# Value products of attention given out behind the next group's transposes, the last operand's product first

## The chip, the cores and the metric

The kernel runs as one program on 1 core of one Trainium2 chip. The metric is the device time of one execution in microseconds (us); the core's five engines (TensorE for matmuls, VectorE, ScalarE, GpSimd, and SyncE, which issues DMAs) run side by side, each through its own queue of instructions in order, and wait for one another through semaphores. In the profile TensorE stands as PE (matmuls) and PEld (its weight loads), VectorE as DVE, ScalarE as ACT, GpSimd as POOL and SyncE as SP.

## The reference

One layer of a decoder with two kinds of attention side by side, 2048 tokens of width 1024, in float32. What the change touches are the two attentions, 8 heads of width 64 each:

```python
# forgetting attention (FoX), F = cumsum(log_sigmoid(forget logits))
s = einsum('bhqd,bhkd->bhqk', q_blk, k) * scale + F_blk[..., None] - F[:, :, None, :]
p = softmax(where(causal, s, -inf))
o_fox = einsum('bhqk,bhkd->bhqd', p, v)

# stick-breaking attention
z = einsum('bhqd,bhkd->bhqk', q_blk, k) * scale
log_one_minus_beta = where(strict, log_sigmoid(-z), 0.0)
rest = cumsum(log_one_minus_beta, axis=3, reverse=True) - log_one_minus_beta
a = where(strict, exp(log_sigmoid(z) + rest), 0.0)
o_sb = einsum('bhqk,bhkd->bhqd', a, v)
```

Around them: a modulated RMSNorm and one input projection that gives q, k and v of both kinds and the forget logits; after them a per-head RMSNorm, the output projection with a gated residual, a gated MLP with a causal convolution of width 3, and a last RMSNorm.

## The kernel before

**Precision.** Operands of matmuls are split into two float32r parts, a high one (a rounded copy) and a low one (what the copy left). A product is the sum of high by high, high by low and low by high, or, where a [high | low] pair is packed into the 128 rows or columns of the array, two matmuls.

**Units.** Attention works through 32 units, `units`: first the stick-breaking kind (`sb`), then the forgetting kind (`fox`); in each, 4 pairs of heads `p`; for each pair, 4 blocks `tb` of 512 queries. `attend` (from L697) runs one unit: two halves `j2` of 256 queries by two heads `hl`, so four passes of one head over 256 queries. `sb_head` (L620) takes the keys in chunks of 512 from the last to the first: per chunk and each of the two rows of 128 queries (`qi` 0 and 1) there are two matmuls for the logits (`logits`, L594, lines L596 and L597), two sigmoids on ScalarE (L630, L631) and one scan on VectorE (L636). `fox_head` (L657) first makes all logits of a row, adds the forget sums and keeps the running minimum on VectorE (L675), and takes the exponential on ScalarE (L679), for `qi` 0 and then 1.

**A group.** Both give their weights to `weighted` (L600), once per group of 256 queries by 256 keys. Its steps: four 128x128 transposes on TensorE into one PSUM bank `pt` of three (L606; three of them in a group on the diagonal); a copy on ScalarE into the high half of an operand tile `at` of three (L610); a subtraction on VectorE into its low half (L611); and four value products on TensorE (L615), for two key tiles `kk` times the high and the low half `w`. On the diagonal ScalarE also fills a quarter of `at` with zeros first (L609). The order of the transposes is `order = [(1, 0), (0, 0), (0, 1), (1, 1)]`, each pair being key tile and query row. The products of all groups of one head add up in one bank `o`: the single bank `pv`, or one of two banks `bc` in the last but one unit. There are 576 groups.

**The end of a head.** When a head's groups are through, ScalarE copies half of `o` to SBUF (L737), VectorE adds the other half to it into `oT` (L738), and after both heads `head_var` squares `oT` on GpSimd (L711) and puts off two variance matmuls (L716) by 13 steps. After both halves SyncE stores `oT` to DRAM.

**The order of work.** The program is traced by generators that yield at each group: `interleave` draws one step of attention, then as many steps of the next units' projections (`project`, lines L342 and L413) as `pace` has due, then fillers such as the modulation's remaining part (`late_mod`, L780 to L790) and, in the last two units, the first part of the output projection (`first_mix`, `first_out`, L912). From this trace a scheduler fixes the order on every engine by a simulated timeline (`schedule_with_timeline_sim=True`): of the instructions whose operands the simulation holds ready, the one traced first is issued. So a product that is traced before the next group's transposes can still stand after them. `tc.issue_after(x)` adds an order on one engine without a wait: what is traced in it stands behind `x` in that engine's queue. `sums` and `step` note the last product and the two copies of a group for such orders later (`behind`, and the first output products of the last stage).

Of the kernel before, what the change touches and what calls it, by code (L numbers as in the profile page):

```python
# [9 lines left out]
F32 = mybir.dt.float32  # L10
F32R = mybir.dt.float32r
BF16 = mybir.dt.bfloat16
AF = mybir.ActivationFunctionType
# [4 lines left out]
P = 128  # L18
# [3 lines left out]
HD = 64  # L22
# [3 lines left out]
NTB = S // TB  # L26
# [8 lines left out]
def kernel(ctx: ExitStack, tc: tile.TileContext, x, c, w_ada, b_ada, g_attn, w_in, b_fgate,  # L35
                      g_out_fox, g_out_sb, w_out, g_mlp, w_up, conv_w, conv_b, w_down, g_final, out):
    nc = tc.nc
# [3 lines left out]
    def f(t):  # L41
        return t.bitcast(F32)
# [9 lines left out]
    os_ = [[dram.tile([P, TB], F32, name=f"os{p}_{t}") for t in range(NTB)] for p in range(NPAIR)]  # L52
# [21 lines left out]
    ident = edge[:, TB - P:TB]  # L74
# [50 lines left out]
    def open_pool(name, side=None, space=None):  # L125
        st = pools[name] = ExitStack()
        kw = dict(space=space) if space is not None else {}
        return st.enter_context(tc.tile_pool(name=name, bufs=1, side=side, reuse_waits="tile", **kw))
# [8 lines left out]
    sb = open_pool("sb", side="right")  # L137
# [3 lines left out]
    def bank(pool, tag, bufs):  # L141
        return pool.tile([P, 512], F32, name=f"ps_{tag}", tag=tag, bufs=bufs)
# [4 lines left out]
    pv = lambda: bank(psb, "pv", 1)  # L147
# [55 lines left out]
    last = {}  # L203
# [13 lines left out]
    b = pv()  # L217
# [37 lines left out]
    class mod_cols:  # L255
# [6 lines left out]
        def add(self, k0, k1):  # L262
            if k0 == 0:
                self.t = px.tile([P, 2, 2 * P], F32, name="adas", tag="z", bufs=2)
                nc.vector.tensor_scalar_mul(self.t, self.w[0], cs[:, 0:1])
            for k in range(max(1, k0), k1):
                nc.vector.scalar_tensor_tensor(self.t, self.w[k], cs[:, k:k + 1], self.t, ALU.mult, ALU.add)
# [326 lines left out]
    def logits(cw, qcols, hl, Q, K):  # L594
# [2 lines left out]
        marks.append(nc.tensor.matmul(b[:, :cw], Q[:, hl, 1, qcols], K[:, hl, :cw], start=False, stop=True).ins)  # L597
        return b

    def weighted(o, kts, blk, V, hl, first, last, diag):  # L600
        b = pt()
        at = sb.tile([P, 2, 2 * 2 * P], F32R, name="at", tag="at", bufs=3)
        order = [(1, 0), (0, 0), (0, 1), (1, 1)]
        for i, (kk, qi) in enumerate(order):
            if not (diag and i == 0):
                nc.tensor.transpose(b[:, i * P:(i + 1) * P], blk(kts[kk], qi), ident)  # L606
        lo = P if diag else 0
        if diag:
            nc.scalar.activation(at[:, :, 0:P], edge[:, 0:2 * P].rearrange("p (a n) -> p a n", n=P), AF.Copy)  # L609
        copies = [nc.scalar.activation(at[:, 0, lo:], b[:, lo:], AF.Copy).ins,  # L610
                  nc.vector.tensor_sub(at[:, 1, lo:], b[:, lo:], f(at[:, 0, lo:])).ins]  # L611
        for kk, kt in enumerate(kts):
            for w in range(2):
                rhs = at[:, w].rearrange("p (s q) -> p s q", q=P)[:, 0:4:3, :] if kk else at[:, w, P:3 * P]
                m = nc.tensor.matmul(o[:, 0:2 * P], V[kt // 4][:, kt % 4, hl, :], rhs,  # L615
                                     start=first and kk == 0 and w == 0, stop=last and kk == 1 and w == 1)
        sums.append(m.ins)
        step[:] = [m.ins] + copies

    def sb_head(j, qc, hl, Q, K, V, o):  # L620
        n = (2 * j + 2 + 3) // 4
        right = [None, None]
        for ch in range(n - 1, -1, -1):
            at = []
            for qi in range(2):
                need = min(512, (2 * j + qi + 1) * P - ch * 512)
                b = logits(max(need, 2 * P), slice((qc + qi) * P, (qc + qi + 1) * P), hl, Q, K[ch])
                r = sx.tile([P, 512], F32, name="r", bufs=7)
                a = sx.tile([P, 512], F32, name="a", bufs=7)
                nc.scalar.activation(r[:, :need], b[:, :need], AF.Sigmoid)  # L630
                nc.scalar.activation(a[:, :need], b[:, :need], AF.Sigmoid, scale=-1.0)  # L631
                if right[qi] is None:
                    nc.gpsimd.affine_select(out=a[:, need - P:need], in_=a[:, need - P:need], pattern=[[-1, P]],
                                            base=-1, channel_multiplier=1, compare_op=ALU.is_ge, fill=0.0)
                rev = a[:, 0:need][:, ::-1]
                nc.vector.tensor_tensor_scan(rev, r[:, 0:need][:, ::-1], rev,  # L636
                                             0.0 if right[qi] is None else right[qi][:, 0:1], ALU.mult, ALU.add)
                right[qi] = a
                at.append(a)
            yield  # L640
            nk = min(4, 2 * j + 2 - 4 * ch)
            for m in range(0, nk, 2):
                kts = [4 * ch + m, 4 * ch + m + 1]
                weighted(o, kts, lambda kt, qi: at[qi][:, (kt - 4 * ch) * P:(kt - 4 * ch + 1) * P], V, hl,
                         ch == n - 1 and m == 0, ch == 0 and m == nk - 2, kts[0] == 2 * j)
                yield
# [40 lines left out]
    sums, step, mask = [], [], []  # L687
# [9 lines left out]
    def attend(kind, p, tb, res, Fbs):  # L697
        Q = res[tb][0]
        K = [r[1] for r in res]
        V = [r[2] for r in res]  # L700
        oT = sb.tile([P, TB], F32, name="oT", bufs=2)
        last_unit = (kind, p, tb) == units[-1]
        if kind == "fox":
            ls = sx.tile([P, 2, 4], F32, name="ls", bufs=2)
        mp = p if kind == "fox" else p + 4

        def head_var(j2):
            sq = (sx.tile([P, 2 * P], F32, name="sq", bufs=1) if kind == "sb" and (p, tb) != (3, NTB - 1) else
                  px.tile([P, TB], F32, name="sq", tag="z", bufs=2)[:, 0:2 * P])
            cols_ = slice(j2 * 2 * P, (j2 + 1) * 2 * P)  # L710
            nc.gpsimd.tensor_mul(sq, oT[:, cols_], oT[:, cols_])  # L711

            def reduce():
                b = bank(psd, "t", 2) if last_unit and j2 else pt()
                for t in range(2):
                    nc.tensor.matmul(b[:, 2 * t:2 * t + 2], sq[:, t * P:(t + 1) * P], headsel, start=True, stop=True)  # L716
                v = var[tb][:, 2 * j2:2 * j2 + 2, 2 * mp:2 * mp + 2]
                bv = b[:, 0:4].rearrange("p (t h) -> p t h", t=2)
                if kind == "fox":
                    l = ls[:, :, 2 * j2:2 * j2 + 2]  # L720
                    nc.vector.scalar_tensor_tensor(l, l, EPS, l, ALU.mult, ALU.mult)
                    nc.vector.scalar_tensor_tensor(v, bv, 1.0 / HD, l.rearrange("p h t -> p t h"), ALU.mult, ALU.add)
                else:
                    nc.vector.tensor_scalar(v, bv, 1.0 / HD, EPS, ALU.mult, ALU.add)

            deferred.append([reduce, 13])

        for j2 in range(2):
            j = 2 * tb + j2
            for hl in range(2):  # L730
                o = bank(psc, "bc", 2) if (kind, p, tb) == units[-2] else pv()
                if kind == "sb":
                    yield from sb_head(j, 2 * j2, hl, Q, K, V, o)
                else:
                    yield from fox_head(j, 2 * j2, hl, Q, K, V, o, Fbs[hl], ls)
                o2 = sb.tile([HD, 2 * P], F32, name="o2", bufs=2)
                step[1] = nc.scalar.activation(o2, o[HD:P, 0:2 * P], AF.Copy).ins  # L737
                nc.vector.tensor_add(oT[hl * HD:(hl + 1) * HD, j2 * 2 * P:(j2 + 1) * 2 * P], o[0:HD, 0:2 * P], o2)  # L738
            head_var(j2)
        nc.sync.dma_start(os_[mp][tb], oT)  # L740
        yield

    def fold_out(gt):
# [63 lines left out]
    units = [(k, p, tb) for k in ("sb", "fox") for p in range(4) for tb in range(NTB)]  # L807
# [222 lines left out]
    for i, u in enumerate(units):  # L1030
        kind, p, tb = u
# [15 lines left out]
        if i == len(units) - 2:  # L1047
# [4 lines left out]
            psc = open_pool("psc", side="right", space=PSUM)  # L1052
# [23 lines left out]
    def chunk(u, c):  # L1076
        t, n, q = ORDER.get(u, TURN)[c]
        if (t, n) not in banks:
            banks[t, n] = bank(psc, "bc", 2) if u == 1 and t == 0 else bank(psd, "o", 4)
        with fixed():  # L1080
            out_matmuls(u, banks[t, n], t, n, q)
        return t, n, q
# [171 lines left out]
    first = {"raw": [], "ws": []}  # L1254
# [41 lines left out]
    for u in range(1, NU):  # L1296
        for c in range(8 if u == 1 else 0, 16):
            t, n, q = chunk(u, c)
# [8 lines left out]
    def bank_a():  # L1307
        return bank(psd, "o", 4)
# [137 lines left out]
    soon, held = [], []  # L1446
    for sblk, order in enumerate(orders):
# [47 lines left out]
        a, b = bank_a(), bank_a()  # L1495
# [189 lines left out]
    for i in range(7):  # L1685
        nxt = {}
        kept = []
        for s in range(2):
# [7 lines left out]
            for kp in range(NKP):  # L1696
# [5 lines left out]
                w = bops[kp]  # L1702
# [60 lines left out]
```

## The time and the profile before

| what | value |
|---|---|
| three runs | 2945.81, 2949.18 (median) and 2950.16 us |
| span of the profiled execution | 2941.4 us, from its first to its last instruction; it is not one of the three runs |
| mean granted TensorE clock | 0.993 of full speed |
| TensorE, matmuls | 2867.8 us, 97% of the span, 15772 instructions |
| TensorE, weight loads | 2459.7 us, 84% |
| VectorE | 2179.5 us, 74% |
| ScalarE | 1686.0 us, 57% |
| GpSimd | 901.1 us, 31% |
| DMA | 601.89 MB, 205 GB/s in the mean |

The first 85 us hold the modulation and the first block's projections, the stretch to about 1520 us the 32 units of attention with the other projections beside them, and the rest the output projection and the MLP. A row of the grouped views names line, engine, operation and the tiles written and read, with the count; behind the bar stand busy time, mean ns of one, and the idle time just before, with the instruction that ended it. A row of the waits names who waited, for whom, and the total, the number and the longest of the waits. A row of the timeline gives start, length, engine, line and count of merged instructions, with the idle time before the first in brackets. Matmuls overlap in a pipeline and their ends are modelled, so the time from start to start tells more of TensorE than the length of one.

### The profile page before, as it was taken

How to read it: one execution, taken by the hardware profiler on the slowest of the kernel's cores; microseconds unless marked ns; L12 is line 12 of the kernel's file. 1: busy time of each engine (PE TensorE's matmuls, PEld its weight loads, DVE VectorE, ACT ScalarE, POOL GpSimd, SP SyncE). 2: the span in 40 equal slices, each digit the busy share in tenths (PEclk: the TensorE clock that was granted, in tenths of full speed). 3: DMA queues.
4: the chain of work that ended last, by engine and by line, in shares of the span. 5: the costliest groups of instructions: out<-in, count | busy, mean ns of one | idle time of the engine just before them, and what ended most of it. 6: DMA issues, size and time to landing. Idle time of an engine off the chain costs nothing.

```text
span 2941.4 us, 45922 instructions
## 1 busy us (share of the span) xinstructions
PE 2867.8 (97%) x15772; PEld 2459.7 (84%) x15772; DVE 2179.5 (74%) x3464; ACT 1686.0 (57%) x3187; POOL 901.1 (31%) x967
## 2 busy tenths in 40 slices
PE   8999999999999999999999999999999999999998
PEld 7888888888988988888888788888788888888887
DVE  5787778877886656658843788888998888575476
ACT  5776767677776656658744554444444445433342
POOL 0431322243032423231213344444254543142200
PEclk8999999999999999999999999999999999999999
DMA  9749756867469794794537775554754444975644
GB/s 293 255 139 321 236 188 207 301 211 229 162 212 356 269 277 139 232 323 140 182 120 233 245 232 128 130 136 129 236 132 125 130 130 132 309 257 185 216 158 151
DMA packets 348346, 601.89 MB, mean 205 GB/s; under 512 B 34672, under 2 KB 178800, under 8 KB 348112
## 3 DMA queue, kind: packets, MB, share of 16 engines
q1 hardware_dynamic: 324208, 558.06, 57.7%
q0 software_dynamic: 10880, 20.97, 4.3%
q10 hardware_dynamic: 13024, 19.93, 1.9%
q8 instruction: 124, 2.03, 0.3%
q14 instruction: 110, 0.90, 0.1%
HBM read 420.77 MB, written 177.02 MB: 203 GB/s over the span
## 4 chain that ended last, share of the span: by engine, by line
PE 46%; DMA 3%; DVE 2%; SPq 1%; ACT 1%; issue 1%; POOL 0%; DVEq 0%; ACTq 0%; POOLq 0%
PE ps_o L1315 19%; PE ps_t L1315 7%; PE ps_o L1614 6%; PE ps_t L1614 3%; PE ps_bc L1614 3%; PE ps_o L912 1%; PE ps_pv L615 1%; DMA r<-rstd 1%; PE ps_bc L912 1%; PE ps_pt L606 1%; PE ps_o L1609 1%; DMA wo<-wos 1%; DMA hm<-hf_m 1%; SPq L895 1%; DVE op L46 1%
## 5 line engine op out<-in xcount | busy, mean ns | idle before, releaser
L1315 PE MATMUL ps_o<-op,wu 128*128 128x512 f32 x2592 | 608.0, 389 | 2.0 <-DVE snap L1366 1.5
L1315 PEld LDWEIGHTS ps_o<-op,wu 128*128 128x128 f32 x2592 | 486.2, 188 | 103.9 <-DVE snap L1366 1.9
L611 DVE TENSOR_TENSOR at<-ps_pt,at 128x512 fp32r<-128x512 f32 (+1 forms) x576 | 366.1, 652 | 100.2 <-ACT at L610 97.3
L636 DVE TENSOR_TENSOR_SCAN a<-r,a 128x512 f32<-128x512 f32 (+2 forms) x320 | 368.3, 1167 | 77.8 <-ACT a L631 39.9
L342 PE MATMUL ps_pj<-hp,w_qk 128*128 128x512 f32 x1512 | 411.2, 403 | 14.5 <-DMA hp<-hs 12.9
L610 ACT ACTIVATE at<-ps_pt 128x512 fp32r<-128x512 f32 (+1 forms) x576 | 318.5, 576 | 139.1 <-PE ps_pt L606 123.1
L615 PE MATMUL ps_pv<-at,V 128*128 128x256 f32 x2216 | 386.8, 292 | 9.3 <-DVE at L611 4.2
L615 PEld LDWEIGHTS ps_pv<-at,V 128*128 128x128 f32 x2216 | 320.9, 190 | 39.8 <-DVE at L611 11.4
L342 PEld LDWEIGHTS ps_pj<-hp,w_qk 128*128 128x128 f32 x1512 | 275.4, 190 | 71.0 <-DMA hp<-hs 16.2
L45 ACT ACTIVATE wu<-wuraw 128x512 fp32r<-128x512 f32 x204 | 128.9, 632 | 248.5 <-PE ps_o L1315 190.1
L596 PE MATMUL ps_qk<-K,Q 128*128 128x512 f32 (+2 forms) x640 | 265.7, 416 | 5.6 <-ACT a L631 3.3
L413 PE MATMUL ps_pj<-w_v,hp 128*128 128x256 f32 (+1 forms) x1536 | 236.6, 288 | 2.1 <-DVE hp L422 1.6
L597 PE MATMUL ps_qk<-K,Q 128*128 128x512 f32 (+2 forms) x640 | 235.7, 369 | 0.0
L1315 PE MATMUL ps_t<-op,wu 128*128 128x512 f32 x888 | 220.8, 390 | 1.0 <-DVE op L46 1.0
L413 PEld LDWEIGHTS ps_pj<-w_v,hp 128*128 128x128 f32 x1536 | 209.0, 189 | 10.9 <-DVE q L373 1.5
L630 ACT ACTIVATE r<-ps_qk 128x512 f32<-128x512 f32 (+2 forms) x320 | 173.1, 541 | 58.2 <-PE ps_qk L597 55.5
L46 DVE TENSOR_TENSOR wu<-wuraw,wu 128x512 fp32r<-128x512 f32 x204 | 189.6, 930 | 18.1 <-ACT wu L45 16.7
L1315 PEld LDWEIGHTS ps_t<-op,wu 128*128 128x128 f32 x888 | 166.4, 188 | 36.5 <-DVE op L46 1.8
L606 PE MATMUL ps_pt<-edge,a 128*128 128x128 f32 x1088 | 185.1, 274 | 8.4 <-DVE a L636 7.8
L1614 PE MATMUL ps_o<-op 128*128 128x512 f32 x840 | 191.5, 389 | 0.0
L1614 PEld LDWEIGHTS ps_o<-op 128*128 128x128 f32 x840 | 157.7, 188 | 32.7
L679 ACT ACTIVATE p<-p,mn 128x128 f32<-128x128 f32 (+15 forms) x128 | 153.9, 1203 | 53.3 <-DVE mn L675 52.2
(342 smaller groups left out, 5237.6 us busy)
## 6 DMA issues: line engine op xcount, KB each, us to landing
hp<-hs SPq DMA_DIRECT2D x224, 512.0 KB
wuraw<-in_w_up_dram SPq DMA_DIRECT2D x80, 512.0 KB
ra<-g SPq DMA_DIRECT2D x136, 256.0 KB
rb<-in_w_down_dram SPq DMA_DIRECT2D x108, 256.0 KB
g<-u SPq DMA_DIRECT2D x80, 256.0 KB
hs<-hp SPq DMA_DIRECT2D x32, 512.0 KB
hp<-in_w_ada_dram SPq DMA_DIRECT2D x32, 512.0 KB
qk_fox<-q SPq DMA_DIRECT2D x32, 512.0 KB
```

Of the source, the lines that this page charges most:

```text
L46: (lo_engine or nc.gpsimd).tensor_sub(lo, src, f(hi))
L342: nc.tensor.matmul(acc, w[kt][:, a, n], h[:, bb], start=kt == 0 and i == 0, stop=kt == KT - 1 and i == 2)
L413: nc.tensor.matmul(av[:, t * width:(t + 1) * width], hts[kt][:, a, tok], w[1][kt][:, bb, 0:width], start=kt == 0 and m == 0, stop=kt == KT ...
L596: nc.tensor.matmul(b[:, :cw], Q[:, hl, 0, qcols], K[:, hl, :cw], start=True, stop=False)
L597: marks.append(nc.tensor.matmul(b[:, :cw], Q[:, hl, 1, qcols], K[:, hl, :cw], start=False, stop=True).ins)
L606: nc.tensor.transpose(b[:, i * P:(i + 1) * P], blk(kts[kk], qi), ident)
L610: copies = [nc.scalar.activation(at[:, 0, lo:], b[:, lo:], AF.Copy).ins, nc.vector.tensor_sub(at[:, 1, lo:], b[:, lo:], f(at[:, 0, lo:])).ins]
L611: nc.vector.tensor_sub(at[:, 1, lo:], b[:, lo:], f(at[:, 0, lo:])).ins]
L615: m = nc.tensor.matmul(o[:, 0:2 * P], V[kt // 4][:, kt % 4, hl, :], rhs, start=first and kk == 0 and w == 0, stop=last and kk == 1 and w == 1)
L636: nc.vector.tensor_tensor_scan(rev, r[:, 0:need][:, ::-1], rev, 0.0 if right[qi] is None else right[qi][:, 0:1], ALU.mult, ALU.add)
L1315: nc.tensor.matmul(b, w[:, p, j], o[:, q], start=first and i == 0, stop=last and i == 2, skip_group_check=True)
L1614: nc.tensor.matmul(b, a[:, p, t * P:(t + 1) * P], w[:, q], start=first and i == 0, stop=last and i == 2, skip_group_check=True)
```

## The change

`weighted` no longer traces its four products at once. It puts them into a list `pend` as a function `add`, and the next call of `weighted`, after its own transposes and copies are traced, runs the list with `flush(m)`, where `m` is that call's last transpose: each product of the earlier group is traced then, the first in order behind `m` and each further one behind the one before it. Within a key tile the low half's product (`w` = 1) comes first and the high half's second. The transposes are traced in the reverse order, (1, 1) first, the others in order behind that first one.

The bank `o` becomes a function that takes its bank at the first product that runs, and the end of a head (L737, L738, the variance and the store of `oT`) goes into the same list behind the head's last products. At the last block of a pair (`tb == NTB - 1`) and in the last three units the list is run at the unit's end; elsewhere it goes over into the next unit.

```diff
+    pend = []
+
+    def flush(lead=None):
+        for fn in pend[:]:
+            lead = fn(lead)
+        pend.clear()
+
     def weighted(o, kts, blk, V, hl, first, last, diag):
         b = pt()
         at = sb.tile([P, 2, 2 * 2 * P], F32R, name="at", tag="at", bufs=3)
         order = [(1, 0), (0, 0), (0, 1), (1, 1)]
-        for i, (kk, qi) in enumerate(order):
+        lead = None
+        for i in (3, 2, 1, 0):
+            kk, qi = order[i]
             if not (diag and i == 0):
-                nc.tensor.transpose(b[:, i * P:(i + 1) * P], blk(kts[kk], qi), ident)
+                with tc.issue_after(lead) if lead else nullcontext():
+                    m = nc.tensor.transpose(b[:, i * P:(i + 1) * P], blk(kts[kk], qi), ident).ins
+                lead = lead or m
...
-        for kk, kt in enumerate(kts):
-            for w in range(2):
-                rhs = at[:, w].rearrange("p (s q) -> p s q", q=P)[:, 0:4:3, :] if kk else at[:, w, P:3 * P]
-                m = nc.tensor.matmul(o[:, 0:2 * P], V[kt // 4][:, kt % 4, hl, :], rhs,
-                                     start=first and kk == 0 and w == 0, stop=last and kk == 1 and w == 1)
-        sums.append(m.ins)
-        step[:] = [m.ins] + copies
+
+        def add(lead):
+            for kk, kt in enumerate(kts):
+                for w in (1, 0):
+                    rhs = at[:, w].rearrange("p (s q) -> p s q", q=P)[:, 0:4:3, :] if kk else at[:, w, P:3 * P]
+                    with tc.issue_after(lead) if lead else nullcontext():
+                        m = nc.tensor.matmul(o()[:, 0:2 * P], V[kt // 4][:, kt % 4, hl, :], rhs,
+                                             start=first and kk == 0 and w == 1, stop=last and kk == 1 and w == 0)
+                    lead = m.ins
+            sums.append(m.ins)
+            step[:] = [m.ins] + copies
+
+        flush(m)
+        pend.append(add)
...
-                o = bank(psc, "bc", 2) if (kind, p, tb) == units[-2] else pv()
+                held = []
+
+                def o(held=held):
+                    if not held:
+                        held.append(bank(psc, "bc", 2) if (kind, p, tb) == units[-2] else pv())
+                    return held[0]
+
...
-                o2 = sb.tile([HD, 2 * P], F32, name="o2", bufs=2)
-                step[1] = nc.scalar.activation(o2, o[HD:P, 0:2 * P], AF.Copy).ins
-                nc.vector.tensor_add(oT[hl * HD:(hl + 1) * HD, j2 * 2 * P:(j2 + 1) * 2 * P], o[0:HD, 0:2 * P], o2)
-            head_var(j2)
-        nc.sync.dma_start(os_[mp][tb], oT)
+
+                def end_head(_, o=o, hl=hl, j2=j2):
+                    o2 = sb.tile([HD, 2 * P], F32, name="o2", bufs=2)
+                    step[1] = nc.scalar.activation(o2, o()[HD:P, 0:2 * P], AF.Copy).ins
+                    nc.vector.tensor_add(oT[hl * HD:(hl + 1) * HD, j2 * 2 * P:(j2 + 1) * 2 * P], o()[0:HD, 0:2 * P], o2)
+                    if hl:
+                        head_var(j2)
+                    if hl and j2:
+                        nc.sync.dma_start(os_[mp][tb], oT)
+
+                pend.append(end_head)
+        if tb == NTB - 1 or (kind, p, tb) in units[-3:]:
+            flush()
         yield
```

## The prediction

> **What bounds the kernel now.** I read the page's engine table first, then the busy time of two stretches, then the waits of TensorE's weight loader within the first, and last the timeline at single waits.
>
> ```profile
> PE 2867.8 (97%) x15772; PEld 2459.7 (84%) x15772; DVE 2179.5 (74%) x3464; ACT 1686.0 (57%) x3187; POOL 901.1 (31%) x967
> ...
> 85.00:1520.00 1435.00, 1389.13 (x9131) 1237.04 (x9129) 1067.11 (x1966) 999.49 (x2054) 404.46 (x526) 0.99 0.68 224
> 1520.00:2942.00 1422.00, 1403.88 (x6236) 1158.17 (x6236) 1057.58 (x1382) 635.34 (x1024) 485.01 (x426) 1.00 0.59 179
> ```
>
> TensorE bounds the kernel: 97% busy over the span. Attention fills the stretch from 85 to 1520 us, where the columns are TensorE, its loader, VectorE, ScalarE and GpSimd; the change touches nothing outside it. VectorE is busy 1067.11 of 1435 us there and ScalarE 999.49, so neither is full. TensorE's gaps show as 1435 - 1389.13 = 45.9 us, but more is hidden: a product's end is modelled 0.28 us after its start while undisturbed products start 0.12 us apart ((0.64 - 0.28) / 3 from the row at 1344.32 below), so a stall under 0.16 us leaves no gap. The loader's waits see more:
>
> ```profile
> PEld ps_pj L342 <- DMA hp<-hs: 16.2, 11, 6.4
> PEld ps_pv L615 <- DVE at L611: 11.4, 27, 1.2
> PEld ps_pt L606 <- DVE a L636: 9.0, 12, 1.7
> ...
> PEld ps_pv L615 <- DVE oT L738: 4.2, 6, 1.6
> PEld ps_pv L615 <- ACT at L610: 4.1, 8, 1.0
> PEld ps_bc L615 <- DVE at L611: 3.5, 8, 1.0
> ...
> PEld ps_pt L606 <- ACT p L679: 3.2, 7, 1.3
> ...
> PEld ps_bc L615 <- ACT at L610: 2.1, 3, 0.8
> ```
>
> Columns: total us, times, longest. The value products (L615) wait 11.4 + 4.2 + 4.1 + 3.5 + 2.1 = 25.3 us in 27 + 6 + 8 + 8 + 3 = 52 waits. The transposes (L606) wait 9.0 + 3.2 = 12.2 us on scans and exponentials in 19. These 37.5 us, 1.3% of the time, are what the change can reach; the 16.2 us of block loads (L342) it cannot.
>
> The timeline shows how one group pays twice:
>
> ```profile
> 654.43 0.58 ACT L610 ACTIVATE at<-ps_pt 128x512 fp32r<-128x512 f32 x1
> 655.04 0.69 DVE L611 TENSOR_TENSOR at<-ps_pt,at 128x512 fp32r<-128x512 f32 x1 [0.25 <-ACT at L610]
> 655.06 0.19 PEld L615 LDWEIGHTS ps_pv<-at,V 128*128 128x128 f32 x1 [0.94 <-ACT at L610]
> 655.06 0.38 PE L615 MATMUL ps_pv<-at,V 128*128 128x256 f32 x1 [0.62 <-ACT at L610]
> 655.78 0.41 PEld L615 LDWEIGHTS ps_pv<-at,V 128*128 128x128 f32 x3 [0.54 <-DVE at L611]
> 655.78 0.62 PE L615 MATMUL ps_pv<-at,V 128*128 128x256 f32 x3 [0.34 <-DVE at L611]
> 656.14 0.25 PEld L606 LDWEIGHTS ps_pt<-edge,a 128*128 128x128 f32 x2
> ```
>
> The first product waits for ScalarE's copy (high part), the next three for VectorE's subtraction (low part); two of the next group's transposes come only after, at 656.14.
>
> **How much of the order is already so.** The change forces a group's products behind the next group's transposes.
>
> ```profile
> L615 PE MATMUL ps_pv<-at,V x2216: 274/282/682, 89.6 to 1514.1; 128*128 128x256 f32 x185
> L615 PE MATMUL ps_bc<-at,V x88: 274/282/389, 1416.2 to 1450.5; 128*128 128x256 f32 x88
> L606 PE MATMUL ps_pt<-edge,a x1088: 270/272/421, 74.7 to 868.0; 128*128 128x128 f32 x182
> L606 PE MATMUL ps_pt<-edge,p x1088: 270/272/421, 872.3 to 1510.6; 128*128 128x128 f32 x182
> L610 ACT ACTIVATE at<-ps_pt x576: 462/597/719, 80.4 to 1512.3; 128x512 fp32r<-128x512 f32 x144, 128x384 fp32r<-128x384 f32 x48
> ```
>
> 2216 + 88 = 2304 products are 4 to each of the 576 copies, and 2176 transposes are 4 or 3 to each, so in order of time each group's parts can be paired. Of the 575 groups that have a next one, 502 already run all four products after its last transpose. In 73 a product comes earlier, from 106.97 us to 1478.54 us, by 60.4 us in all (first such product to the last transpose of the next group). So most of the new order exists; what is new in most groups is that the four products stay together behind one wait. Before, the first is parted from the second in 337 groups, and the transposes of a group are parted in 206.
>
> **The change part by part.** No matmul, copy or DMA is added or dropped.
>
> a) The product bank. The single `pv` bank is refilled only after the sum of the head before (L738) has read it. Afterwards the next head's first products come a whole group later. All 4.2 us go; bounds 0 and 4.2.
>
> b) Low product first. A group now waits once, for VectorE. The 4.1 + 2.1 = 6.2 us on ScalarE vanish as waits, but as the group at 655 shows, a group can then wait for VectorE anyway. I take half, 3.1 us; bounds 0 and 6.2.
>
> c) The waits for VectorE, 11.4 + 3.5 = 14.9 us. A product sits at the point in TensorE's order where the scheduler's simulated timeline holds its operand ready; the wait is how late the real operand is. That lateness stays, but the products are now traced behind the next group's transposes and whatever logits and projection steps come between, so they drop behind that work wherever it is ready. I take half, 7.5 us; bounds 0 and 14.9.
>
> d) Restarts. An undisturbed run of four, a run of transposes, and a run of four that waited:
>
> ```profile
> 1344.32 0.64 PE L615 MATMUL ps_pv<-at,V 128*128 128x256 f32 x4
> ...
> 1346.06 0.81 PE L606 MATMUL ps_pt<-edge,p 128*128 128x128 f32 x6
> ...
> 633.20 0.74 PE L615 MATMUL ps_pv<-at,V 128*128 128x256 f32 x4 [0.62 <-DVE at L611]
> ```
>
> A wait costs 0.10 us beyond itself, and the row at 655.06 says why: the weight load begins only with the waiting product. If 52 waits become 25, 27 x 0.10 = 2.7 us go; bounds 0 and 5.2. The Trainium skill (page "TensorE: Matmul & The Clock Gate", section "Part 2: What happens when you issue a matmul") has TensorE pull weight loads ahead of matmuls in flight; by that rule the weights would be in before the wait ends, this term would be 0 and the sum 2.7 us smaller. The trace does not bear it out at a waiting product.
>
> e) Transposes, last operand first. The first transpose now needs the later scan or exponential. The end of the wait is the same as that of the second half before; the two transposes that used to run ahead of it now run after. Bounds: all 12.2 us gained, or 19 waits x 2 transposes x 0.11 us ((0.81 - 0.27) / 5 from the row of six at 1346.06) = 4.2 us lost. I take 0, nearest to the loss, since no scan ends earlier.
>
> ```profile
> 1460.69 0.64 PE L615 MATMUL ps_pv<-at,V 128*128 128x256 f32 x4
> ...
> 1462.43 1.55 PE L912 MATMUL ps_bc<-wo,mix 128*128 128x512 f32 x6
> ...
> L342 PE MATMUL ps_pj<-hp,w_qk x1512: 387/393/988, 26.3 to 1324.1; 128*128 128x512 f32 x189
> ```
>
> f) The 73 displaced groups. Their products must now let other work go first. The cover is projection matmuls (L342), which run until 1324.1 us, and logits. Ten of the 73, 8.7 us, lie later, as those at 1460.69; there output products (L912) cover some. Without any cover it costs 60.4 us; I take 2, a quarter of the uncovered part.
>
> g) The operand buffers. `at` has three. From a group's copy to its last product's end it is held 4.7 us in the mean over the 576 (first copy at 80.4, last at 1512.3, in the row above); three buffers at one group in (1512.3 - 80.4) / 575 = 2.49 us allow 7.5 us. ScalarE already waits for them:
>
> ```profile
> ACT at L609 <- PE ps_pv L615: 22.4, 17, 3.3
> ...
> ACT at L610 <- PE ps_pv L615: 10.3, 13, 1.9
> ```
>
> Behind such a wait stand the sigmoids and exponentials in ScalarE's queue, then the scans, then the transposes. The waits are 22.4 + 10.3 = 32.7 us; the products' forced order lengthens the mean hold by 60.4 / 576 = 0.1 us. I charge 1 us; bounds 0 and a doubling, 32.7.
>
> h) The end of a head (L737, L738) moves behind the next head's first transposes. ScalarE is 70% busy in this stretch (999.49 of 1435 us) and can wait there; of TensorE's work only a) waits on it. The head's variance and, per unit, one DMA of `oT` on SP's queue come a group later; neither is read before the output stage except by the variance matmuls, put off by 13 steps already. At the end of each pair and in the last three units all is given out at once as before. Cost 0; without that cover, a late `oT` store would hold its two buffers, and VectorE's sum with them.
>
> What is late next: TensorE, sooner past a product, meets the next scan sooner. Of the 9.0 us at L636 I let waits grow by a quarter, 2.5 us.
>
> Sum: -4.2 - 3.1 - 7.5 - 2.7 + 0 + 2 + 1 + 2.5 = -12.0 us. On the profiled span, 2941.4 - 12.0 = 2929.4 us. The three runs have a median of 2949.18, 7.8 us over the span, which lies outside it and does not change; so 2937 us.
>
> **The rivals.**
>
> 1. The waits only move: same time. For it: 502 of 575 groups already stand in the new order, so slack hardly grows; VectorE is as late as before, so c) gives 0 and e) loses 4.2. Then, with d) at 1, -4.2 - 3.1 - 1 + 4.2 + 2 + 1 + 2.5 = +1.4 us, 2951 us. Against it: the paired waits as at 655 and the bank's 4.2 us end in any case.
>
> 2. Slower: the operand buffers run out. If products drop further behind projection steps than the forced order demands, the hold passes 7.5 us often, and ScalarE's 32.7 us at L609 and L610 grow. It decides once over 12 us of added waits reach TensorE. A doubling that reaches it whole, in place of the 1 us in g), gives -12.0 - 1 + 32.7 = +19.7 us, 2969 us; half of it, -12.0 - 1 + 16.4 = +3.4 us, 2953 us. For it: 17 and 13 such waits exist, and a tenth of the groups already hold a buffer over 6.7 us. Against it: ScalarE has 30% idle time in this stretch. The Trainium skill (page "Perfetto Trace Analysis", section "Optimization Strategy") reads a repeated gap on an engine as a possible want of buffers for the next tile, which is this mechanism.
>
> 3. Slower: displaced products find no cover. All of f) gives 60.4 - 2 - 12.0 = +46.4 us, 2996 us. Against it: projection steps run beside 63 of the 73.
>
> 4. More than forecast: a) to d) at their upper bounds, 4.2 + 6.2 + 14.9 + 5.2 = 30.5 us, less 2 + 1 + 2.5, gives 2924 us; with a third of e), 2920.
>
> **How the numbers follow.** The forecast gets 0.42, with an own range of 2927 to 2943; rival 4 gets 0.13, rival 1 0.23, rival 2 0.17, rival 3 0.05. About 0.2%, 5.9 us, is what a measurement of this kernel can tell from no change. Faster: 0.42 + 0.13 = 0.55; same 0.23; slower 0.17 + 0.05 = 0.22. The range from 2918 to 2960 holds the forecast, rival 4, rival 1 and the smaller half of rival 2, some 0.85 in all, and leaves out the doubling and rival 3.
>
> **What would show it.** In the changed profile: the loader's wait of products on `oT` near 0 (a); on ScalarE's copy near 0 (b); on VectorE some 7 us, not 14.9 (c); products in runs of four, and the sum of the L606 waits between 8 and 16 us (e); ScalarE's waits at L609 and L610 near 33 us (g). TensorE's busy time from 85 us to the last product should stay, and the stage end some 12 us sooner. The forecast is wrong if ScalarE's buffer waits pass 45 us, if transposes wait over 20 us, or if the stage after 1520 changes length, which this reasoning does not allow; chance shifts of the block loads' 16.2 us could hide or double the gain.

## The result and the profile after

The changed kernel takes 2969.68 us (median of 5 runs, 2964.81 to 2971.43) against 2949.18 us: a ratio of 1.0071, 95% interval [1.0059, 1.0083]. It is slower by 20.5 us, where 12 us less was forecast, and lies outside the range from 2918 to 2960 us.

In the page's engine table and in the busy time by stretch, TensorE does the same work in a longer stretch. The stretches go from the first logits to a fixed matmul of the output projection, from there to the first MLP matmul, and to the end.

```profile
PE 2870.8 (97%) x15772; PEld 2463.5 (83%) x15772; DVE 2182.2 (74%) x3464; ACT 1685.7 (57%) x3188; POOL 902.2 (30%) x967
...
72.60:1553.00 1480.40, 1419.08 (x9289) 1263.25 (x9288) 1090.22 (x1993) 1021.31 (x2103) 413.55 (x539) 0.99 0.67 223
1553.00:1686.20 133.20, 129.94 (x606) 105.87 (x604) 62.76 (x109) 61.48 (x136) 40.85 (x47) 1.00 0.75 248
1686.20:2963.10 1276.90, 1258.62 (x5551) 1039.04 (x5549) 988.68 (x1263) 566.89 (x875) 447.12 (x375) 1.00 0.59 171
```

The same three stretches of the kernel before:

```profile
69.90:1537.70 1467.80, 1420.24 (x9287) 1262.22 (x9288) 1085.64 (x1989) 1019.81 (x2101) 418.42 (x539) 0.99 0.68 225
1537.70:1670.90 133.20, 129.99 (x607) 105.91 (x605) 63.28 (x112) 62.68 (x136) 42.19 (x47) 1.00 0.75 250
1670.90:2941.40 1270.50, 1256.81 (x5551) 1038.29 (x5549) 989.20 (x1260) 566.28 (x875) 439.82 (x375) 1.00 0.58 172
```

The span grew by 2963.1 - 2941.4 = 21.7 us: 2.7 before the first logits, 12.6 in attention, 0 in the output stage, 6.4 in the MLP. TensorE's busy time in attention is 1.2 us less, so the 12.6 us are waiting. Who waits, for the weight loader of the changed kernel between 85 and 1535 us (total us, times, longest; L629 is the products' line now, L616 that of the transposes, L622 VectorE's subtraction, L654 the scan, L697 the exponential, L764 the head's sum, L693 the running minimum and L649 the second sigmoid):

```profile
PEld ps_pv L629 <- DVE at L622: 17.3, 29, 3.0
PEld ps_pj L342 <- DMA hp<-hs: 11.8, 8, 5.1
PEld ps_qk L596 <- DVE mn L693: 10.8, 23, 2.0
PEld ps_pt L616 <- ACT p L697: 8.4, 12, 1.5
PEld ps_qk L596 <- ACT a L649: 6.4, 6, 2.8
...
PEld ps_pv L629 <- DVE oT L764: 5.5, 9, 2.5
PEld ps_pt L616 <- DVE a L654: 4.7, 5, 2.0
...
PEld ps_bc L629 <- DVE at L622: 1.8, 5, 0.6
```

The products wait 17.3 + 5.5 + 1.8 = 24.6 us in 43 waits, against 25.3 us in 52: nothing is gained, and the longest grew from 1.6 (on the head's sum) to 3.0 us. The waits for ScalarE's copy are gone, those for VectorE rose from 14.9 to 19.1. ScalarE's waits for an `at` buffer rose from 32.7 to 25.6 + 24.4 + 1.0 = 51.0 us (L620 is the zero fill of a quarter of the tile, L621 the copy):

```profile
ACT at L620 <- PE ps_pv L629: 25.6, 21, 4.3
ACT at L621 <- PE ps_pv L629: 24.4, 18, 4.8
...
ACT at L620 <- PE ps_bc L629: 1.0, 1, 1.0
```

The longest wait of a product shows where one comes from. Three views of the changed kernel near 865 us, the timeline first, then the busy time and granted clock (third number from the end) of two short stretches:

```profile
859.74 0.60 ACT L621 ACTIVATE at<-ps_pt 128x512 fp32r<-128x512 f32 x1 [1.11 <-PE ps_pt L616]
860.66 0.60 ACT L621 ACTIVATE at<-ps_pt 128x512 fp32r<-128x512 f32 x1 [0.32 <-PE ps_pt L616]
...
863.56 1.41 DVE L781 SCALAR_TENSOR_TENSOR hp<-hp,cols 128x512 f32<-128x512 f32 x2 [3.42 <-DMA hp<-in_w_out_dram]
864.89 1.28 DVE L622 TENSOR_TENSOR at<-ps_pt,at 128x512 fp32r<-128x512 f32 x2
865.63 0.93 PEld L629 LDWEIGHTS ps_pv<-at,V 128*128 128x128 f32 x4 [3.01 <-DVE at L622]
865.63 1.22 PE L629 MATMUL ps_pv<-at,V 128*128 128x256 f32 x4 [2.81 <-DVE at L622]
...
862.00:865.00 3.00, 0.82 (x8) 0.61 (x6) 1.44 (x3) 0.90 (x3) 0.00 (x0) 1.00 1.03 259
865.00:868.50 3.50, 2.87 (x13) 2.87 (x14) 3.50 (x4) 2.82 (x6) 3.22 (x2) 0.52 1.06 247
```

The order of VectorE's queue has two operations of the output weights (L781) ahead of the subtractions of two groups. Their DMA lands late and VectorE stands 3.42 us. The subtractions behind them stand too, though ScalarE's copies that they read were done at 860.34 and 861.26 us, and TensorE's loader waits 3.01 us for the first. Then TensorE's clock is granted at 0.52 for the next 3.5 us, and four products take 1.22 us, not 0.64. Nothing in this chain belongs to the change but the place of L622 in a queue.

### The profile page after: what moved, and what is told of

It reads as the page before. It is cut to its first block, busy times and chain, and to the rows that moved or that the text cites. A ratio compares the mean times of both kernels' runs of the same rounds, so it can differ in the third digit from the quotient of the medians.

```text
span 2963.1 us, 45901 instructions
## 1 busy us (share of the span) xinstructions
PE 2870.8 (97%) x15772; PEld 2463.5 (83%) x15772; DVE 2182.2 (74%) x3464; ACT 1685.7 (57%) x3188; POOL 902.2 (30%) x967
## 4 chain that ended last, share of the span: by engine, by line
PE 70%; DMA 15%; DVE 5%; ACT 3%; issue 3%; SPq 2%; POOL 2%; ACTq 0%; DVEq 0%; POOLq 0%
PE ps_o L1347 20%; PE ps_pj L342 8%; PE ps_t L1347 8%; PE ps_pv L629 6%; PE ps_o L1646 5%; PE ps_pt L616 5%; PE ps_pj L413 4%; PE ps_qk L596 3%; PE ps_qk L597 3%; DMA hp<-hs 2%; PE ps_t L1646 2%; PE ps_bc L1646 2%; DMA r<-rstd 1%; DMA hp<-in_w_ada_dram 1%; DVE a L654 1%
## 5 line engine op out<-in xcount | busy, mean ns | idle before, releaser
L622 DVE TENSOR_TENSOR at<-ps_pt,at 128x512 fp32r<-128x512 f32 (+1 forms) x576 | 366.4, 651 | 116.2 <-ACT at L621 114.0
L654 DVE TENSOR_TENSOR_SCAN a<-r,a 128x512 f32<-128x512 f32 (+2 forms) x320 | 372.7, 1184 | 86.2 <-POOL a L651 47.6
L342 PE MATMUL ps_pj<-hp,w_qk 128*128 128x512 f32 x1512 | 410.2, 403 | 12.3 <-DMA hp<-hs 9.1
L621 ACT ACTIVATE at<-ps_pt 128x512 fp32r<-128x512 f32 (+1 forms) x576 | 322.0, 575 | 167.7 <-PE ps_pt L616 133.9
L629 PE MATMUL ps_pv<-at,V 128*128 128x256 f32 x2216 | 358.5, 291 | 13.2 <-DVE at L622 9.1
L629 PEld LDWEIGHTS ps_pv<-at,V 128*128 128x128 f32 x2216 | 305.9, 190 | 36.7 <-DVE at L622 17.3
L596 PE MATMUL ps_qk<-K,Q 128*128 128x512 f32 (+2 forms) x640 | 256.3, 402 | 9.6 <-ACT a L649 5.4
L597 PE MATMUL ps_qk<-K,Q 128*128 128x512 f32 (+2 forms) x640 | 234.0, 368 | 0.0
L413 PE MATMUL ps_pj<-w_v,hp 128*128 128x256 f32 (+1 forms) x1536 | 228.9, 287 | 2.1 <-DVE hp L422 1.6
L46 DVE TENSOR_TENSOR wu<-wuraw,wu 128x512 fp32r<-128x512 f32 x204 | 189.2, 927 | 19.1 <-ACT wu L45 17.9
L697 ACT ACTIVATE p<-p,mn 128x128 f32<-128x128 f32 (+15 forms) x128 | 153.8, 1202 | 57.0 <-DVE mn L693 55.9
L616 PE MATMUL ps_pt<-edge,a 128*128 128x128 f32 x1088 | 165.2, 274 | 13.2 <-DVE a L654 6.8
```

Source lines behind the costliest of these rows:

```text
L46: (lo_engine or nc.gpsimd).tensor_sub(lo, src, f(hi))
L342: nc.tensor.matmul(acc, w[kt][:, a, n], h[:, bb], start=kt == 0 and i == 0, stop=kt == KT - 1 and i == 2)
L413: nc.tensor.matmul(av[:, t * width:(t + 1) * width], hts[kt][:, a, tok], w[1][kt][:, bb, 0:width], start=kt == 0 and m == 0, stop=kt == KT ...
L596: nc.tensor.matmul(b[:, :cw], Q[:, hl, 0, qcols], K[:, hl, :cw], start=True, stop=False)
L616: m = nc.tensor.transpose(b[:, i * P:(i + 1) * P], blk(kts[kk], qi), ident).ins
L629: m = nc.tensor.matmul(o()[:, 0:2 * P], V[kt // 4][:, kt % 4, hl, :], rhs, start=first and kk == 0 and w == 1, stop=last and kk == 1 and w ...
```

## The experiments

Theory A was rival 2, too few `at` buffers; theory B, that asking for the last operand first costs by itself; theory C, that the scheduler draws a new plan for all five queues from any edit, and that the time is set by where that plan meets late operands. "Waits" are the product waits of the loader and their number, and ScalarE's waits for `at`, between 85 and 1560 us, from one profile of each. The change has one product wait more than in the rows above, 0.2 us for the zero fill.

| run | median us | ratio [95%] | products' waits, us/times | `at` waits, us |
|---|---|---|---|---|
| before | 2949.18 | 1 | 25.3/52 | 32.7 |
| the change | 2969.68 | 1.0071 [1.0059, 1.0083] | 24.8/44 | 51.0 |
| e1 transposes alone | 2962.46 | 1.0048 [1.0033, 1.0063] | 26.6/45 | 38.0 |
| e2 low first alone | 2961.11 | 1.0039 [1.0025, 1.0053] | 24.3/45 | 35.3 |
| e3 deferral alone | 2979.57 | 1.0103 [1.0086, 1.0120] | 20.6/41 | 55.6 |
| e4 change, four `at` | 2980.35 | 1.0111 [1.0092, 1.0130] | 20.2/34 | 16.2 |
| e5 old plan, low first | 2952.13 | 1.0015 [1.0003, 1.0027] | 30.5/47 | 31.7 |
| e6 old plan, deferral too | 2955.68 | 1.0025 [1.0012, 1.0038] | 30.3/46 | 31.8 |
| e7 before, variance 14 | 2977.49 | 1.0110 [1.0091, 1.0128] | 25.4/53 | 44.7 |
| e8 before, pace 0.79 | 2973.40 | 1.0090 [1.0067, 1.0113] | 41.5/59 | 38.3 |
| e9 before, LAG 13 | 2951.55 | 1.0010 [1.0000, 1.0020] | 20.6/48 | 34.7 |
| e10 old plan, later runs | 2949.87 | 1.0010 [0.9998, 1.0021] | 21.6/45 | 32.9 |
| a11 change, variance 14 | 2969.36 | 1.0064 [1.0045, 1.0083] | 19.3/40 | 35.6 |
| a12 change, pace 0.79 | 2959.14 | 1.0032 [1.0021, 1.0043] | 23.6/41 | 50.8 |
| a13 change, LAG 13 | 2964.36 | 1.0041 [1.0025, 1.0057] | 19.9/38 | 54.8 |
| a14 before, variance 12 | 2974.75 | 1.0087 [1.0067, 1.0107] | 26.1/47 | 41.0 |

**One part of the change at a time (e1 to e3).**

```diff
 # e1: transposes as in the change, products and ends of heads as before
+        lead = None
+        for i in (3, 2, 1, 0):
...
 # e2: low half's product first, all else as before
-            for w in range(2):
+            for w in (1, 0):
...
 # e3: the deferral (pend, flush, end_head) as in the change, but
+        for i, (kk, qi) in enumerate(order):   # old order of the transposes
+                for w in range(2):             # high half first
```

> The kernel before with one part of the change alone: the transposes in the reverse order, the first one needing the later operand and the others queued behind it. Theory A, operand buffers (the deferred products hold `at` longer, ScalarE waits for a buffer and everything behind it comes late): the products stay where they were, so no change, 2943 to 2955 us, ScalarE's waits at the two `at` lines near 33 us. Theory B, one late wait (asking for the last operand first takes from TensorE the two transposes it could run before it): slower by 6 to 15 us, 2955 to 2964 us, with the loader's waits of the transposes on scans and exponentials over 12.2 us. Theory C (any new order meets the real lateness of operands at other places): anywhere within 2940 to 2965 us.

> The kernel before with one part of the change alone: in each key tile the low half's product before the high half's, so that a group's products wait once, for VectorE. Theory A: no change, 2943 to 2955 us. Theory B: the product that could run after ScalarE's copy now waits for VectorE as well, slower by 3 to 10 us, 2952 to 2960 us; the waits of products on VectorE rise from 14.9 us to 20 us or more while those on ScalarE go. Theory C: 2940 to 2965 us.

> The change without its two reversals: products and the ends of heads are given out behind the next group's transposes, in the old order (high half first, transposes from (1, 0) on). Theory A: the loss is here, 2960 to 2972 us, and ScalarE's waits for `at` are 45 us or more as after the change (50 us against 32.7 before). Theory B: no loss or a gain, 2935 to 2952 us, as products have more slack. Theory C: 2940 to 2965 us.

Each part alone is slower, by 12.3, 10.9 and 29.4 us, and the three together lose less than the third alone. Theory A has no place for e1 and e2, theory B none for e3. Theory B came near the time of both e1 and e2, and e2's waits for VectorE did rise to 22.2 us while those for ScalarE went; but e1's waits of transposes on scans and exponentials fell, from 12.2 to 8.1 us, where they were to rise. e3 lies above every range that was named, theory C's too. The losses do not add up, which theory C allows.

**More buffers (e4).**

```diff
-        at = sb.tile([P, 2, 2 * 2 * P], F32R, name="at", tag="at", bufs=3)
+        at = sb.tile([P, 2, 2 * 2 * P], F32R, name="at", tag="at", bufs=4)
...
-    o2 = sb.tile(..., name="o2", bufs=2)      oT = sb.tile(..., name="oT", bufs=2)
+    o2 = sb.tile(..., name="o2", bufs=1)      oT = sb.tile(..., name="oT", bufs=1)
...
```

> The whole change with four `at` buffers in place of three; the room comes from one `o2` and one `oT` buffer in place of two each, and from one small tile that shares another's place. Theory A: ScalarE's waits for `at` fall well below 33 us and the time comes back to 2940 to 2952 us. Theory B: the waits for `at` fall and the time stays at 2960 to 2972 us. Theory C: any time between, unrelated to the waits for `at`.

ScalarE's waits for `at` in that run:

```profile
ACT at L620 <- PE ps_pv L629: 9.1, 7, 4.5
ACT at L621 <- PE ps_pv L629: 7.1, 7, 2.2
```

They fall from 51.0 to 16.2 us, half of what the kernel before has, and the time is 2980.35 us, above every range that was named. Rival 2 named 2969 us, almost the measured time of the change, and its waits did grow past the 45 us it set; but taking them away did not bring the time back, so that agreement may be luck. They are no sufficient account of the loss. That they cost nothing is not shown: e4 has a plan of its own and one `oT` buffer.

**The old plan held (e5, e6).** At the end of the trace each queue's instructions are chained in a list written into the kernel, so that only what the list changes is changed: e5, e6 and e10 differ from one another in TensorE's list alone, and in their traces VectorE's 3464 instructions stand in the order of the kernel before. In outline:

```diff
+    for queue in QUEUES:                       # five lists of instructions, one for each engine
+        for prev, name in zip(queue, queue[1:]):
+            tc.add_manual_dep(by[name], prev, ...)   # order only, no wait
 # e5: w in (1, 0), and in TensorE's list each group's four products at the second one's place
 # e6: and 14 groups' products moved behind the next group's last transpose
```

> The order of all five queues is written out as the kernel before has it, and one thing is changed in it: each group's four products stand together, low half first, at the place where the second of them stood. This is the low-first part of the change without the new plan that the scheduler makes of everything else. If the loss of the low-first part alone (2961 us) is a cost of the one late wait: 2955 us or more. If it is the new plan that costs: 2940 to 2953 us, with the products' waits on ScalarE gone and those on VectorE near 15 us.

> As the run before in this set, and besides, inside a head, the 14 groups' products that stood ahead of the next group's last transpose are moved behind it (42 at the ends of heads stay, since ScalarE's queue holds the end of the head ahead of what those transposes need). The order of everything else is that of the kernel before. If the deferral itself costs: 2960 us or more. If the new plan costs: 2940 to 2953 us.

The loader's waits of e5:

```profile
PEld ps_pv L615 <- DVE at L611: 20.6, 32, 2.5
...
PEld ps_bc L615 <- DVE at L611: 5.6, 10, 1.5
PEld ps_pv L615 <- DVE oT L738: 4.3, 5, 1.9
```

With everything else in its place, low first costs 0.15%, and with the part of the deferral that can be tried it is 0.25% in all: 3 and 7 us of loss, not 21, with intervals from 1 to 8 and from 4 to 11 us. e5 falls in the range for a cost of the new plan, though its waits for VectorE were to stay near 15 us; e6 falls between its two ranges. The products of e5 wait 20.6 + 5.6 = 26.2 us for VectorE, against 14.9 for VectorE and 6.2 for ScalarE before: the first product, which used to run early, no longer fills a part of the wait for the second. The reversed transposes were not tried in the old plan, and the deferral over the end of a head could not be: ScalarE's queue holds the head's end ahead of what the next head's transposes need.

**New plans without a reason (e7 to e9, a14).**

```diff
-            deferred.append([reduce, 13])
+            deferred.append([reduce, 14])      # e7; 12 in a14
-            yield max(first + (due - first) * min(1.0, m / (0.8 * n)),
+            yield max(first + (due - first) * min(1.0, m / (0.79 * n)),   # e8
...
-    LAG, ENDQ = 12, 16
+    LAG, ENDQ = 13, 16                         # e9
```

> The kernel before with its variance matmuls put off by 14 steps in place of 13: 64 pairs of small matmuls stand one step later, which by itself moves no operand that anything waits for. The scheduler makes a new plan from it. If the time of a plan is a matter of where the order meets late operands, it is slower by 4 to 20 us, 2954 to 2970 us, with TensorE's stalls spread over all lines. If plans are alike and the change's own parts cost: 2944 to 2954 us.

> The kernel before with the projection steps due a little earlier (0.79 of a unit's steps in place of 0.8). The same two expectations as for the run before it: 2954 to 2970 us if a new plan costs by itself, 2944 to 2954 us if it does not.

> The kernel before with the projections of the first units queued behind the logits 13 back in place of 12 (LAG), a third edit that moves no operand that anything waits for by more than one step. If a new plan costs by itself: 2954 to 2980 us. If the two edits before it were chance: 2944 to 2954 us.

> The kernel before with its variance matmuls put off by 12 steps in place of 13. If plans differ by chance: 2945 to 2980 us, most likely over 2950 us, since of three such edits none was faster. If 28 us at 14 steps came from the lateness of the variance itself: 2945 to 2953 us.

Four edits that touch none of what the change touches cost 28.6, 24.5, 1.7 and 25.8 us, and the variance put off by one step more or by one less costs alike. e7 and e8 lie above the 2954 to 2970 us named for a cost of the plan, and e9 in the range named for chance, so a new plan can cost much or almost nothing. How far the plans part can be counted in the traces, by operation and tile names: some 820 of VectorE's 3464 instructions stand elsewhere than before in e7, 490 in e9, 570 in e2, whose edit names TensorE's products alone, and 1190 in the changed kernel. Where the time goes differs from plan to plan. The row of waits that grew most in e7, and then that in e8:

```profile
PEld ps_pt L606 <- DVE a L636: 16.2, 18, 1.9
```

```profile
PEld ps_pv L615 <- DVE oT L738: 13.4, 7, 6.9
```

In e7 transposes wait for scans (16.2 us against 9.0), in e8 products wait for the head's sum (13.4 against 4.2, one of them 6.9 us long).

A part of the loss is the granted clock. Span and mean clock of four profiles, in the order before, the change, e7, e8:

```profile
core 0: 2941.4 us, clock 0.993
core 0: 2963.1 us, clock 0.991
core 0: 2981.8 us, clock 0.989
core 0: 2982.8 us, clock 0.985
```

Span times what the clock lacks of 1 gives 21, 27, 33 and 45 us; so at most 6 of the change's 21.7 us, 12 of e7's 40.4 and 24 of e8's 41.4 are clock (estimates, as if TensorE had been busy all the while). The profiled executions of e7 and e8 are longer than their medians; over all their executions the mean clock is 0.987 and 0.988, beside 0.991 for the kernel before. It is not the whole account: e2's mean is 0.991 too, and it is 10.9 us slower.

**Products and transposes moved away from their waits (e10).**

```diff
 # e10: in TensorE's list of the kernel before, 36 runs of products or transposes that had waited
 #      over 0.15 us stand behind the projections or logits that followed them
```

> All queues in the written-out order of the kernel before, high half first, nothing deferred; only in TensorE's queue 36 runs of products or transposes that waited over 0.15 us in the profile of before are moved behind the projections or logits that follow them, enough to cover 14 us of their waits. If what counts is where the order meets late operands, it gains 4 to 14 us: 2935 to 2945 us. If TensorE only meets the next late operand sooner: 2946 to 2954 us. If the projections brought forward are late themselves: over 2954 us.

The loader's waits of e10, and the two rows on logits of the kernel before:

```profile
PEld ps_pv L615 <- DVE at L611: 11.4, 25, 1.5
PEld ps_qk L596 <- ACT a L631: 10.9, 15, 1.9
...
PEld ps_qk L596 <- DVE mn L675: 7.9, 19, 1.1
...
PEld ps_pt L606 <- DVE a L636: 4.5, 7, 1.5
...
PEld ps_pt L606 <- ACT p L679: 3.1, 6, 1.1
```

```profile
PEld ps_qk L596 <- ACT a L631: 5.8, 10, 1.3
PEld ps_qk L596 <- DVE mn L675: 5.2, 14, 0.8
```

The transposes wait 4.5 + 3.1 = 7.6 us where they waited 12.2, and the products 21.6 where they waited 25.3. The logits wait 10.9 + 7.9 = 18.8 us where they waited 11.0. What was taken from these lines, 8.3 us, others have in its place, 7.8 us, and the time stays, in the range named for the next late operand met sooner.

**The same edits on the changed kernel (a11 to a13).**

> The whole change, and the variance matmuls put off by 14 steps in place of 13, the edit that cost the kernel before 28 us. If the plan decides and the change itself costs 3 to 7 us: anywhere from 2950 to 2985 us, unrelated to the 2969.7 us of the change alone. If the change itself costs 20 us: 2965 us or more.

> The whole change, and the projection steps due at 0.79 in place of 0.8, the edit that cost the kernel before 24 us. If the plan decides: 2950 to 2985 us. If the change itself costs 20 us: 2965 us or more.

> The whole change, and the projections queued behind the logits 13 back in place of 12, the edit that cost the kernel before 2 us. If the plan decides: 2950 to 2985 us. If the change itself costs 20 us: 2965 us or more.

Two of the three lie below 2965 us, one of them by 0.6 us only, and the third fits both readings. The edits that cost the kernel before 28.6 and 24.5 us changed the time of the changed one by -0.3 and -10.5 us. Over the plans that were run, the kernel before stands at ratios of 1, 1.0110, 1.0090, 1.0010 and 1.0087, 1.0059 in the mean; the changed kernel at 1.0071, 1.0064, 1.0032 and 1.0041, 1.0052 in the mean. The two ranges overlap, and with so few plans a difference under some half a per cent between them could not be seen. No version was faster than the kernel before.

So what could be tried of the change in the old order costs 3 to 7 of the 20.5 us. That the rest belongs to the plan is argued, not shown by itself: edits that have no bearing on it cost as much, and over several plans the changed kernel is no slower than the kernel before; but the reversed transposes and the deferral over a head's end were never run in the old order. The kernel before has the best of its five plans. Why is open: the runs show that the plans differ, not what makes a plan good, and it was not tried whether its constants (13, 0.8, 12) are ones that happen to draw a fast plan.

## Why the prediction was wrong, step by step

The step that failed is the premise under the whole sum, that every other instruction stays where it stood, so that the waits at the touched lines can be taken off one by one. Among the terms it shows most in c) and in what is late next.

- **a) the product bank**: 4.2 us were to go; the rows show 5.5 us in 9 waits. The next head's products come later, but so does the sum they wait for; what held it up was not followed row by row.
- **b) low first**: right as to the row (no wait for ScalarE's copy is left), wrong as to the gain; in e5 the wait comes back whole on VectorE, 26.2 us against 14.9 + 6.2 = 21.1.
- **c) slack for the products**: this is the term of the sum that failed. 14.9 us were to become 7.4; they became 19.1. A later place in the simulated order does not make the real operand less late when the queue that makes it has a new order as well; that is shown at the wait near 865 us, and argued for the others.
- **d) restarts**: 52 waits became 43, not 25; 0.9 us by its own price, not 2.7.
- **e) transposes**: 8.4 + 4.7 = 13.1 us on scans and exponentials against 12.2, within the 8 to 16 that it gave. With their other waits, among them those for VectorE to free a PSUM bank, the transposes wait 26.9 us against 19.6, which it did not see.
- **f) the displaced groups**: as described; in the changed kernel 3 groups, not 73, run a product ahead of the next group's last transpose. Of its price only e6 tells a part: 14 groups moved, 2952.13 to 2955.68 us, with intervals that overlap.
- **g) the buffers**: the mean time that a group holds its buffer grew by 0.2 us, not 0.1 (4.7 to 4.9, paired as in the prediction), and the waits are 51.0 us where 33.7 were allowed, past the 45 us set as the mark of rival 2. In e4 they fell to 16.2 us and the time did not come back, though with a plan of its own.
- **What is late next** was sized at 2.5 us. In e10 nearly all that was saved came back as waits of other lines, so there this term was nearly as large as the savings. That is the second term that failed. Rival 1 had this mechanism, but its 2951 us were missed as well.
- **What the sum left out**: a new order of all five queues stood at nothing, without a reason. Waits on a plan were read as a property of the lines that the change touches; e7, e8 and a14 show that 24 to 29 us can come from an edit that touches none of them. The remark that shifts of the block loads could hide the gain was the nearest to it, and it had no price in the range. The clock had no term either: by the estimate above it is up to 6 us between the two profiles.
- **The stage after 1520** was not to change; its stretch to the end grew by 6.4 us. One wait of the loader on VectorE at 2138.7 us takes 4.53, where the longest on the same operands near there took 1.39 before. In the profiles of the other kernels, none of which edits this stretch, the time from the first MLP matmul to the end of the last matmul lay between 1258.7 and 1266.1 us (1260.0 in the kernel before), in the changed one at 1266.4, so it varies without the change.
- **The level**: 7.8 us were put around the span. The profiled execution of the changed kernel took 2964.81 us with a span of 2963.1, so it is 1.7 us; by the same 1.7 us the profiled execution of before took some 2943 us, under the three times shown, and the 7.8 us held the distance to the median as well.

## What to carry to other kernels

When a scheduler places every instruction, an edit is measured together with the new plan that it draws: run a few harmless edits first, and take their spread (here 2 to 29 us) as the error of any gain that is read from one plan. To know what the edit itself does, hold the old order and change only the edit. And the waits of a few tenths of a microsecond at one line of an engine that is 97% busy were no sum to be collected here: look for what made the operand late, which can be an unrelated transfer in another engine's queue.

## What the runs showed of the hardware

A wait of TensorE of 2.81 us was followed by 3.5 us at a granted clock of 0.52, in which four products took 1.22 us in place of 0.64; so this wait cost some 1.7 us more (an estimate, 3.5 x 0.48). Not every such wait does: at 1659.3 us of the same profile TensorE stood 2.86 us, and the clock stayed at 1.00 in the 3.8 us behind it. The Trainium skill (page "TensorE: Matmul & The Clock Gate", section "Part 1: The HAM clock gate (the "warmup" mystery)") has the clock fall after an idle window of about 3.4 us; the row at 865.63 us differs, since 2.81 us of idle time were enough here. One late transfer reaches an engine that has no use for it: VectorE stood 3.42 us for a block of output weights, the subtraction behind it stood with its operands ready, and TensorE's loader waited 3.01 us for that subtraction.
